# Hybrid decoder layer on one core: down groups added to x2 in DRAM by accumulating DMAs, and the gate of two up groups 15 products later

## The chip, the cores and the metric

The kernel runs on one core of a Trainium2 chip. The metric is the device time of one execution in microseconds (us). The engines are named as the profile names them: PE (TensorE, with PEld for its weight loads), DVE (VectorE), ACT (ScalarE), POOL (GpSimd) and SP (SyncE, which here only issues DMAs). Each engine runs its own instructions in the order of the program, and waits for others by semaphores.

## The reference

One layer of a decoder: sequence 512, width 2048, all float32. The first half (a combined projection, attention heads and SSD heads, an output projection) is not touched by the change. What matters here is the second half:

```
x = x + concat(attn, ssm) @ w_out                      # this sum is "x2" below
h = rms_norm(x, norm2_w)
u = causal_dwconv(h @ w_up, ffn_conv_w, ffn_conv_b)    # w_up: 2048 x (2 * 5632), conv of 3 taps
u_gate, u_val = split(u, 2)
return x + (silu(u_gate) * u_val) @ w_down             # w_down: 5632 x 2048
```

## The kernel before, in words

Everything is held transposed, with channels on the 128 partitions and the 512 positions along the free axis. x2 consists of 16 tiles of 128 x 512. Each is stored to DRAM when it is made (`x2d`, line 919), because it is needed again at the very end.

Each large product of the second half is computed twice over with a trick. First, every float32 operand is split into a rounded part `hi` (ACT copies and rounds, lines 1088 and 1145) and the rest `lo` (DVE subtracts, lines 1097 and 1146), and a product is hi*hi + hi*lo + lo*hi on PE (lines 1372, 1373, 1375). Second, blocks of 2 x 2 are multiplied by a Strassen-Winograd scheme: seven products, named P1 to P7, instead of eight. So a **group** is seven products of one 256-row block of output channels with both halves of the positions. It needs four weight tiles (DMAs by SP, line 1056), three sums of them on DVE (`s1`, `s2`, `s4`: lines 1067, 1070/1077, 1075) and one on POOL (`s3`, line 1063), and for each product one hi and one lo. A product is 24 matmuls of 128 x 256 where the contraction has 8 chunks, and 21 where it has 7.

The list `items` sets the order of the program by hand. For each group gi it runs P5(gi), P3(gi-1), P1(gi), P4(gi-1), P6(gi), P2(gi), P7(gi). The index of a product in this list is its **slot**. Work on the other engines is hung on slots by `at(slot, ...)`: `events` run before the lo of that slot, `after` behind it. In slot k the program issues the product, then what uses its result (`up_after` or `down_after`), the lo of product k+2, the work of `after`, and the hi of product k+3.

There are 44 **up groups** (0 to 43; each gives the gate channels and the value channels of one block of 128), and then 24 **down groups** in three passes of 8 (m = 0 to 7). Pass 0 contracts over the first 7 pairs of up blocks, pass 1 over the next 8, pass 2 over the last 7.

- `up_after` copies three of the products from PSUM with ACT (line 1227, tile `cP`) and adds the others with DVE. `up_side` then hangs the **gate** of the group on its slot t0 = slot of P4: two multiplies by the RMS factor (lines 1267, 1268), the convolutions (line 1246), the product (line 1257), and for each second group the Winograd sums of the pair (lines 890, 892, 893) and its store to DRAM (`gd`).
- At the start of a pass the right-hand operands of its products come back from `gd`: 14 loads into tiles `ld` (`b_load`, line 1134), each split into hi and lo (`b_split`, lines 1145 and 1146, tile `cmb`), 14 splits within 14 slots. Base is the slot of P5 of the group before the pass. In pass 0 there are three `ld` buffers, later five.
- `down_acc` allocates the accumulator of a down group (128 x 2 x 512) and loads into it x2 (pass 0, line 1284) or what the pass before left in DRAM (`pd`, line 1286). `down_after` adds each of the seven products into it with DVE straight from PSUM (line 1212). After P4 SP stores it to `pd`, or to the output in pass 2.
- Before the first up product, two right-hand operands (K22 and KT4) are still to be made from `xd` in DRAM: four loads (`x_load`, tile `ld`) and four splits (`x_split`, lines 1189 and 1190), at slots 2, 4, 5 and 6.

Of the kernel before, what the change touches and what calls it, by code (L numbers as in the profile page):

```python
# [187 lines left out]
def body(ctx, tc, xT, wi, wz, wo, wu, wd0, wd1, wd2, pp, pf, outT, dbg={}):  # L188
# [688 lines left out]

    x2d = [dram.tile([128, S], F32, name="x2d%d" % j) for j in range(NK)]
    xd = dram.tile([128, 8, 2, 256], F32, name="xd")
# [23 lines left out]
    def g_x2(acc, i):  # L903
# [14 lines left out]
        A_.activation(g[:, o:o + 2, :].rearrange("p a b -> p (a b)"), t, AF.Copy, scale=pc("nw2", j))  # L918
        nc.sync.dma_start(x2d[j], t)

# [10 lines left out]
        else:  # L931
# [10 lines left out]
            kind(KT3)  # L942
        yield
        square(t, i)
        if i + 4 < NK:
# [160 lines left out]
    for gi in range(len(groups)):  # L1106
# [6 lines left out]
        if gi:  # L1113
            at(p5 - 3 if gi > 1 else 1, add, gi, "s1", where=after)
            at(p5 - 3 if gi > 1 else 1, add, gi, "s3", where=after)
        else:
            at(0, add, gi, "s3", where=after)
# [37 lines left out]
    for p in range(len(PASSES)):  # L1155
# [10 lines left out]
        if p == 0:  # L1166
            at(base + 19, down_pool, where=after)

# [8 lines left out]
    def x_load(n):  # L1177
        if n < 4:
            x_ld.append(side_tile(box["pool"], [4, 256], "ld", 3))
            sy.dma_start(x_ld[n], xd[:, 4 * (n % 2):4 * (n % 2) + 4, n // 2, :])  # L1180
# [14 lines left out]

    for n, slot in enumerate((2, 4, 5, 6)):
        at(slot, x_split, n)


    box = {}  # L1200
    pds = [[dram.tile([128, 2, S], F32, name="pd%d_%d" % (p, m)) for m in range(8)] for p in range(2)]

    def down_after(g, x):
# [6 lines left out]
        if x == "P2":  # L1210
            src = src[:, lo]
        ve.tensor_tensor(a[:, row, half], src, a[:, row, half], op=op)  # L1212
        if g is groups[-1]:
            done = {"P7": (1, hi), "P3": (0, slice(0, S)), "P4": (1, lo)}.get(x)
            if done:
                sy.dma_start(outT[2 * g["m"] + done[0]][:, done[1]], a[:, done[0], done[1]])
        elif x == "P4":
            m, p = g["m"], g["p"]
            dst = pds[p][m] if p < 2 else outT[2 * m:2 * m + 2].rearrange("t p s -> p t s")
            at(pos[groups.index(g), "P4"] + 1, sy.dma_start, dst, a)  # L1220

# [16 lines left out]
    def up_side(i, ug, uv):  # L1238
# [20 lines left out]
        def t_sums(n):  # L1259
            sums(ve, box["gt"], n)  # L1260
            if n:
                pr = i // 2
                p = max(q for q in range(3) if PASSES[q][0] <= pr)
                at(t0 + (11 if i < NF - 1 else 9), sy.dma_start, gd[p][:, pr - PASSES[p][0]], box["gt"])

        t0 = pos[i, "P4"]
        for d, fn in ((0, lambda: ve.tensor_tensor(ug[:, 2:514], ug[:, 2:514], rbc, op=OP.mult)),
# [7 lines left out]
    def down_acc(gi):  # L1275
        g = groups[gi]
        m, p = g["m"], g["p"]
        if gi < NF + 2:
            a = g["acc"] = side_tile(lp, [2, S], "acc_s", 2)
        else:  # L1280
            a = g["acc"] = side_tile(box["pool"], [2, S], "acc", 4)
        if p == 0:
            for j in range(2):
                sy.dma_start(a[:, j, :], x2d[2 * m + j])
        else:
            sy.dma_start(a, pds[p - 1][m])

    for gi, g in enumerate(groups):
        if g["ph"] == "down":
            p5 = pos[gi, "P5"]  # L1290
            at(p5 - 2 if gi == NF else p5 - 5 if gi == NF + 1 else p5 - 2 if gi == NF + 2 else p5 - 6, down_acc, gi,
               where=after)

# [3 lines left out]
    def start_up():  # L1297
# [5 lines left out]
        for n in ("ug0", "uv0", "ug1", "uv1"):  # L1303
            box[n] = box["pool"].tile([128, 516], F32, name=n)
            ve.memset(box[n][:, 0:2], 0.0)
        x_load(0), x_load(1), x_load(2)

# [21 lines left out]
    p2["par"] = lp.tile([128, NPF], F32, name="par2")  # L1329
    sy.dma_start(p2["par"], pf)  # L1330
    last = g_x2(last_acc[0], NK - 1)
    split(1), split_lo(1)
# [13 lines left out]
    split_lo(3)  # L1346
    for _ in last:
        pass
    for k, (gi, x) in enumerate(items):
# [58 lines left out]
```

## Time and profile before

| | |
|---|---|
| median of the runs | 2079.29 us (3 runs, 2077.68 to 2079.3) |
| profiled execution, its own time | 2081.46 us |
| its span | 2079.7 us, granted clock 0.997 |
| busy: PE / DVE / ACT / POOL | 98% / 76% / 48% / 10% of the span |
| first half (span 0 to about 781 us) | not touched |
| up groups | about 781 to 1605 us |
| down passes 0, 1, 2 | from about 1622, 1775 and 1933 us |

How to read it: each engine's busy time is a share of the whole span. A wait is put down to the instruction that ended it. A stretch ("window") is given in us from the start of the span. In the rows of DVE one instruction begins a little before the end of the one before it is recorded, so the cost of one in a full queue is the distance from its start to the next start, which is about 0.08 us less than the duration shown.

### The profile page before, as it was taken

Reading aid. Unit: us, or ns where it says so; the run is one execution under the profiler, and the core shown is the slowest. Engines: PE = TensorE matmul, PEld = TensorE weight load, DVE = VectorE, ACT = ScalarE, POOL = GpSimd, SP = SyncE. Lnnn points to the kernel's source line nnn. Section 1 sums busy time; section 2 is a strip of 40 time slices with the busy share of each in tenths; the row PEclk is TensorE's granted clock in tenths of the full one; section 3 lists DMA queues with packets and bytes.
Section 4 is the critical chain, followed back from the end, with each engine's and each line's share of the span. In section 5 each row is a group of like instructions: output and inputs, shape, how many; then the busy total and the mean of one; then the engine's idle time right before and its main releaser. Section 6 shows DMA issues by size and latency. Waiting matters only on the chain.

```text
span 2079.7 us, 37702 instructions
## 1 busy us (share of the span) xinstructions
PE 2046.6 (98%) x15366; PEld 1932.4 (93%) x15366; DVE 1581.4 (76%) x2261; ACT 996.4 (48%) x1437; POOL 205.7 (10%) x108
## 2 busy tenths in 40 slices
PE   9999999999999999999999999999999899999999
PEld 7889888888888889999999999999999799999999
DVE  6545555345565558999999999999999977977976
ACT  6433435244444445555555555555555534634533
POOL 0020000000000001111111011101111111111110
PEclk9999999999999999999999999999999999999999
DMA  5233222332224556444444454454446667756763
GB/s 190 83 109 93 79 71 72 101 102 82 82 72 146 172 169 216 162 158 167 173 173 162 154 189 156 151 184 164 161 163 215 214 218 249 276 179 235 265 203 122
DMA packets 114684, 329.23 MB, mean 158 GB/s; under 512 B 10768, under 2 KB 35152, under 8 KB 111696
## 3 DMA queue, kind: packets, MB, share of 16 engines
q1 hardware_dynamic: 114512, 326.83, 46.9%
q8 instruction: 120, 1.97, 0.4%
q14 instruction: 52, 0.43, 0.1%
HBM read 284.81 MB, written 41.98 MB: 157 GB/s over the span
## 4 chain that ended last, share of the span: by engine, by line
PE 90%; DVE 5%; DMA 2%; issue 1%; ACT 1%; SPq 0%; POOL 0%; DVEq 0%; ACTq 0%; POOLq 0%
PE acc L183 30%; PE x L1373 16%; PE x L1372 16%; PE x L1375 16%; PE sm L183 4%; PE y L1373 3%; PE y L1375 3%; PE y L1372 3%; PE x L1364 2%; DVE lo L1097 1%; DVE cmb L1146 1%; DMA ld<-gd 1%; DMA t<-xT 1%; DVE lo L183 0%; DVE s L1067 0%
## 5 line engine op out<-in xcount | busy, mean ns | idle before, releaser
L1373 PE MATMUL x<-cmb,hi 128*128 128x256 f32 x3054 | 717.3, 278 | 9.9 <-DVE cmb L1146 9.9
L1372 PE MATMUL x<-cmb,hi 128*128 128x256 f32 x3054 | 717.4, 278 | 7.3 <-DVE acc L1212 2.7
L1373 PEld LDWEIGHTS x<-cmb,hi 128*128 128x128 f32 x3054 | 575.3, 188 | 12.1 <-DVE cmb L1146 12.0
L1372 PEld LDWEIGHTS x<-cmb,hi 128*128 128x128 f32 x3054 | 575.2, 188 | 8.9 <-issue 4.1
L1375 PE MATMUL x<-cmb,lo 128*128 128x256 f32 x3054 | 413.2, 277 | 1.9 <-DVE lo L1097 1.8
L1375 PEld LDWEIGHTS x<-cmb,lo 128*128 128x128 f32 x3054 | 377.6, 188 | 2.7 <-DVE lo L1097 2.7
L183 DVE TENSOR_TENSOR lo<-raw,hi 128x512 fp32r<-128x512 f32 (+1 forms) x240 | 164.4, 691 | 230.0 <-ACT hi L183 213.3
L1088 ACT ACTIVATE hi<-s 128x1024 fp32r<-128x1024 f32 (+1 forms) x201 | 201.0, 1000 | 285.2 <-DVE s L1067 192.3
L183 PE MATMUL acc<-A,hi 128*128 128x512 f32 x704 | 278.9, 396 | 1.8 <-ACT hi L183 1.8
L1063 POOL TENSOR_TENSOR rawb<-rawa,rawb 128x1024 f32<-128x1024 f32 (+1 forms) x67 | 167.3, 2497 | 1101.2 <-DVE s L1067 1066.7
L183 PE MATMUL acc<-A,lo 128*128 128x512 f32 x704 | 275.3, 391 | 0.1
L183 PE MATMUL acc<-B,hi 128*128 128x512 f32 x704 | 274.5, 390 | 0.0
L183 ACT ACTIVATE hi<-raw 128x512 fp32r<-128x512 f32 (+1 forms) x240 | 150.0, 629 | 239.1 <-PE acc L183 202.6
L1097 DVE TENSOR_TENSOR lo<-s,hi 128x1024 fp32r<-128x1024 f32 (+1 forms) x201 | 238.1, 1185 | 15.5 <-issue 14.0
L1097 DVE TENSOR_TENSOR lo<-rawa,hi 128x1024 fp32r<-128x1024 f32 (+1 forms) x203 | 240.1, 1183 | 0.0
L1088 ACT ACTIVATE hi<-rawa 128x1024 fp32r<-128x1024 f32 (+1 forms) x203 | 208.7, 1029 | 38.0 <-PE x L1373 37.9
L183 PEld LDWEIGHTS acc<-A,lo 128*128 128x128 f32 x704 | 132.2, 188 | 29.8 <-DVE lo L183 1.8
L183 PEld LDWEIGHTS acc<-A,hi 128*128 128x128 f32 x704 | 132.5, 188 | 28.1 <-ACT hi L183 2.7
L183 PEld LDWEIGHTS acc<-B,hi 128*128 128x128 f32 x704 | 132.4, 188 | 25.9 <-DVE B L183 0.3
L1227 ACT ACTIVATE cP<-x 128x256 f32<-128x256 f32 x132 | 50.6, 384 | 198.1 <-PE x L1375 198.1
L183 PE MATMUL acc<-hi,A 128*128 128x256 f32 (+2 forms) x448 | 135.5, 302 | 0.7 <-DVE u L183 0.7
L183 PE MATMUL acc<-lo,A 128*128 128x256 f32 (+2 forms) x448 | 133.5, 298 | 0.0
(224 smaller groups left out, 2884.0 us busy)
## 6 DMA issues: line engine op xcount, KB each, us to landing
rawa<-wu SPq DMA_DIRECT2D x175, 512.0 KB, 3.7
raw<-wi SPq DMA_DIRECT2D x79, 512.0 KB, 3.6
rawa<-wd SPq DMA_DIRECT2D x64, 448.0 KB, 4.2
rawb<-wu SPq DMA_DIRECT2D x44, 512.0 KB, 4.5
gd<-gt SPq DMA_DIRECT2D x22, 1024.0 KB, 4.6
raw<-wo SPq DMA_DIRECT2D x32, 512.0 KB, 3.5
rawa<-wd SPq DMA_DIRECT2D x32, 512.0 KB, 4.1
ld<-gd SPq DMA_DIRECT2D x27, 512.0 KB, 5.9
```

Source lines behind the costliest of these rows:

```text
L183: return fn(out, *args, **kw)
L1063: (po if gi else ve).tensor_tensor(r, raw[gi, "11"][:, :n], r, op=OP.subtract)
L1088: se.activation(h[:, :n], src[:, :n], AF.Copy)
L1097: ve.tensor_tensor(l[:, :n], src[:, :n], h[:, :n].bitcast(F32), op=OP.subtract)
L1146: ve.tensor_tensor(lo, ld[:, :m, :], hi.bitcast(F32), op=OP.subtract)
L1227: se.activation(g[x], X[:, 256:] if x == "P5" else X[:, :256], AF.Copy)
L1364: pe.matmul(out, a[:, q * 128:(q + 1) * 128], b[:, q, :], start=False, stop=last and q == n - 1, skip_group_check=True)
L1372: pe.matmul(out, w, bk[:, 0, q, :], start=fresh and q == 0, stop=False, skip_group_check=True)
L1373: pe.matmul(out, w, bk[:, 1, q, :], start=False, stop=False, skip_group_check=True)
L1375: pe.matmul(out, l[:, q * 128:(q + 1) * 128], bk[:, 0, q, :], start=False, stop=q == n - 1, skip_group_check=True)
```

## The change

- **Deposits.** `x2d` becomes 8 tiles of 128 x 2 x 512, one for each m. The `pd` tiles go. For the down groups of passes 0 and 1 and for m = 0, 1, 2 of pass 2 (19 groups, `DEPOSIT`), nothing is loaded into the accumulator. The products that come first into a quarter of it (P5, P1, P6, P4) are copied from PSUM by ACT, and P2, P7, P3 are added by DVE as before. After P4 a DMA issued from POOL with `accum_op=add` adds the accumulator to `x2d[m]` in DRAM. For the three groups of pass 2 SP then copies `x2d[m]` to the output, DRAM to DRAM, six slots after P4. The last five groups of pass 2 load `x2d[m]`, add all seven products with DVE, and store to the output.
- **Gate.** For up groups 42 and 43, t0 is 15 slots later. Pair 21, which they form, is read in pass 2 only.
- **Buffers.** Because the up pool now lives until base + 36 (before: base + 19), the accumulators of the first five down groups come from tiles of the long-lived pool (`acc_s`) and, for the third, from an `ld` tile of the up pool.
- **Start of the up groups.** The first `x_load` goes into an `acc_s` tile and is issued before the last x2 tile is finished; its split moves from slot 2 to slot 3. The last square for the RMS sum goes through PSUM, and its add on DVE moves behind slot 2. `s3` of group 1 on POOL moves from slot 1 to slot 7.

```diff
-    x2d = [dram.tile([128, S], F32, name="x2d%d" % j) for j in range(NK)]
+    x2d = [dram.tile([128, 2, S], F32, name="x2d%d" % j) for j in range(NK // 2)]
...
+        if i == NK - 1:
+            q = box["ps"].tile([128, 512], F32, name="y")
+            A_.activation(q, t, AF.Square)
+            yield
+            V.tensor_tensor(p2["ssq"], p2["ssq"], q, op=OP.add)
+            return
         square(t, i)
...
-            at(p5 - 3 if gi > 1 else 1, add, gi, "s3", where=after)
+            at(p5 - 3 if gi > 1 else 7, add, gi, "s3", where=after)
...
-            at(base + 19, down_pool, where=after)
+            at(base + 36, down_pool, where=after)
...
-            x_ld.append(side_tile(box["pool"], [4, 256], "ld", 3))
+            x_ld.append(side_tile(box["pool"], [4, 256], "ld", 3) if n else side_tile(lp, [4, 256], "acc_s", 2))
...
-    for n, slot in enumerate((2, 4, 5, 6)):
+    for n, slot in enumerate((3, 4, 5, 6)):
         at(slot, x_split, n)
...
-    pds = [[dram.tile([128, 2, S], F32, name="pd%d_%d" % (p, m)) for m in range(8)] for p in range(2)]
+    DEPOSIT = lambda g: g["p"] < 2 or g["m"] < 3
...
-        ve.tensor_tensor(a[:, row, half], src, a[:, row, half], op=op)
+        if DEPOSIT(g) and x in ("P5", "P1", "P6", "P4"):
+            se.activation(a[:, row, half], src, AF.Copy)
+        else:
+            ve.tensor_tensor(a[:, row, half], src, a[:, row, half], op=op)
...
-            m, p = g["m"], g["p"]
-            dst = pds[p][m] if p < 2 else outT[2 * m:2 * m + 2].rearrange("t p s -> p t s")
-            at(pos[groups.index(g), "P4"] + 1, sy.dma_start, dst, a)
+            m, end = g["m"], pos[groups.index(g), "P4"]
+            out = outT[2 * m:2 * m + 2].rearrange("t p s -> p t s")
+            if DEPOSIT(g):
+                po.dma_start(x2d[m], a, accum_op=OP.add)
+                if g["p"] == 2:
+                    at(end + 6, sy.dma_start, out, x2d[m])
+            else:
+                at(end + 1, sy.dma_start, out, a)
...
-                at(t0 + (11 if i < NF - 1 else 9), sy.dma_start, gd[p][:, pr - PASSES[p][0]], box["gt"])
+                at(t0 + (11 if i < NF - 1 else 10), sy.dma_start, gd[p][:, pr - PASSES[p][0]], box["gt"])
 
-        t0 = pos[i, "P4"]
+        t0 = pos[i, "P4"] + (15 if i >= NF - 2 else 0)
...
-        if gi < NF + 2:
+        if gi < NF + 5 and gi != NF + 2:
             a = g["acc"] = side_tile(lp, [2, S], "acc_s", 2)
+        elif gi == NF + 2:
+            a = g["acc"] = side_tile(box["pool"], [2, S], "ld", 3)
         else:
             a = g["acc"] = side_tile(box["pool"], [2, S], "acc", 4)
-        if p == 0:
-            for j in range(2):
-                sy.dma_start(a[:, j, :], x2d[2 * m + j])
-        else:
-            sy.dma_start(a, pds[p - 1][m])
+        if not DEPOSIT(g):
+            sy.dma_start(a, x2d[m])
...
-        x_load(0), x_load(1), x_load(2)
+        x_load(1), x_load(2)
...
     sy.dma_start(p2["par"], pf)
+    x_load(0)
```

Three places show how the order on the engines moves. The first is DVE at the start of pass 0, from the lo of a weight sum to the first split of the fourth operand (KT1 to KT4 and K11 to K22 are the tiles `cmb`; `tg`, `tv`, `gt`, `ug`, `uv` belong to the gate; `acc_s` is a down accumulator). Before:

```order
L1212 TENSOR_TENSOR acc_s<-x,acc_s 128x256
L1075 TENSOR_TENSOR s<-s,rawa 128x896
L1097 TENSOR_TENSOR lo_17607<-rawa,hi_17580 128x896
L1146 TENSOR_TENSOR cmb_17534<-ld,cmb_17534 128x768
L1246 SCALAR_TENSOR_TENSOR tg<-ug_7204,par_7109,tg 128x512
L1233 TENSOR_TENSOR ug_7208<-x,cP_17489 128x256
L1097 TENSOR_TENSOR lo_17641<-rawa,hi_17612 128x1024
L1146 TENSOR_TENSOR cmb_17643<-ld,cmb_17643 128x1024
L1246 SCALAR_TENSOR_TENSOR tv<-uv_7206,par_7109,tv 128x512
L1212 TENSOR_TENSOR acc_s<-x,acc_s 128x256
L1097 TENSOR_TENSOR lo_17678<-s,hi_17650 128x896
L1146 TENSOR_TENSOR cmb_17643<-ld,cmb_17643 128x768
```

Two gate rows and two accumulator rows stand among the weights' lo and the operand splits. The same stretch of DVE in the changed kernel (line numbers there are 6 to 14 higher):

```order
L1081 TENSOR_TENSOR s<-s,rawa 128x896
L1103 TENSOR_TENSOR lo_17576<-rawa,hi_17549 128x896
L1152 TENSOR_TENSOR cmb_17508<-ld,cmb_17508 128x768
L1247 TENSOR_TENSOR ug_7185<-x,cP_17464 128x256
L1103 TENSOR_TENSOR lo_17609<-rawa,hi_17580 128x1024
L1152 TENSOR_TENSOR cmb_17611<-ld,cmb_17611 128x1024
L1103 TENSOR_TENSOR lo_17642<-s,hi_17614 128x896
L1152 TENSOR_TENSOR cmb_17611<-ld,cmb_17611 128x768
```

The two rows of `tg` and `tv` and the two of `acc_s` are gone from here; the gate rows stand behind the last split of the pass, and the two accumulator rows are ACT copies.

The second place is POOL in pass 0 of the changed kernel, where before there are only the `s3` rows (rawb<-rawa,rawb):

```order
L1069 TENSOR_TENSOR rawb<-rawa,rawb 128x896 x2
L1230 DMA x2d_140<-acc_s 128x1024
L1069 TENSOR_TENSOR rawb<-rawa,rawb 128x896
L1230 DMA x2d_141<-acc_s 128x1024
L1069 TENSOR_TENSOR rawb<-rawa,rawb 128x896
L1230 DMA x2d_142<-ld 128x1024
```

Between each two `s3` there is now one accumulating DMA, and the `s3` that follows it belongs to the group that starts three slots later.

The third place is ACT at the start of the up groups (`cP` are copies of products, `cmb` is the first operand made by `x_split`). Before:

```order
L1088 ACTIVATE hi_7228<-rawb 128x1024
L1189 ACTIVATE cmb_7259<-ld 128x1024
L1088 ACTIVATE hi_7266<-s 128x1024
L1227 ACTIVATE cP_7292<-x 128x256
L1088 ACTIVATE hi_7299<-acc_s 128x1024
```

In the changed kernel:

```order
L1094 ACTIVATE hi_7202<-rawb 128x1024
L1094 ACTIVATE hi_7235<-s 128x1024
L1241 ACTIVATE cP_7261<-x 128x256
L1195 ACTIVATE cmb_7267<-acc_s 128x1024
L1094 ACTIVATE hi_7274<-acc_s 128x1024
```

The split of the first operand, which reads what a DMA brings, has gone from ahead of a hi and a copy to behind them.

More of the change, by code (lines that the diff above doesn't have):

```diff
@@ L918, in g_x2 @@
         A_.activation(g[:, o:o + 2, :].rearrange("p a b -> p (a b)"), t, AF.Copy, scale=pc("nw2", j))
-        nc.sync.dma_start(x2d[j], t)
+        nc.sync.dma_start(x2d[j // 2][:, j % 2], t)
         def kind(k):
@@ L1290, in body @@
             p5 = pos[gi, "P5"]
-            at(p5 - 2 if gi == NF else p5 - 5 if gi == NF + 1 else p5 - 2 if gi == NF + 2 else p5 - 6, down_acc, gi,
-               where=after)
+            at(p5 - (1 if DEPOSIT(g) else 6), down_acc, gi, where=after)
     up_stack = ExitStack()
@@ L1346, in body @@
     split_lo(3)
-    for _ in last:
-        pass
+    next(last)
+    at(2, lambda: list(last), where=after)
     for k, (gi, x) in enumerate(items):
```

## The prediction

> **What bounds the kernel now.** I read the page's busy times first, then the stretches, then what PE and DVE waited for, then DVE's groups in one stretch.
>
> ```profile
> PE 2046.6 (98%) x15366; PEld 1932.4 (93%) x15366; DVE 1581.4 (76%) x2261; ACT 996.4 (48%) x1437; POOL 205.7 (10%) x108
> ```
>
> PE is the bound, so only time in which PE starves can be won. The stretches show where that is (PE busy with its matmuls, PEld, DVE, ACT, POOL, granted clock, DMA share, GB/s):
>
> ```profile
> 1440.00:1520.00 80.00, 80.00 (x708) 80.00 (x707) 75.48 (x94) 40.68 (x53) 9.83 (x4) 1.00 0.46 158
> 780.00:820.00 40.00, 37.66 (x319) 37.22 (x319) 34.90 (x46) 23.23 (x31) 6.88 (x4) 1.00 0.68 237
> 1600.00:1680.00 80.00, 68.16 (x542) 65.38 (x542) 74.26 (x96) 43.77 (x52) 9.40 (x3) 0.96 0.62 212
> 1760.00:1820.00 60.00, 56.65 (x470) 55.74 (x469) 55.02 (x65) 35.27 (x36) 10.04 (x3) 0.97 0.75 260
> 1920.00:1980.00 60.00, 57.12 (x488) 56.09 (x487) 54.50 (x69) 33.05 (x37) 8.70 (x3) 1.00 0.74 245
> 1840.00:1920.00 80.00, 80.00 (x707) 80.00 (x706) 59.71 (x72) 31.83 (x31) 9.62 (x4) 1.00 0.64 219
> ```
>
> The first row is PE at its pace: 708 matmuls in 80 us, 0.113 us each. I count what is missing at that pace, which takes in the slower matmuls around a wait. Start of pass 0: 708 - 542 = 166, or **18.8 us**. Pass 1: 531 - 470 = 61, **6.9 us**. Pass 2: 531 - 488 = 43, **4.9 us**. Start of the up groups: 354 - 319 = 35, of which some five are the twice as long matmuls of the stage before, **3.4 us**. Together 34.0 us; elsewhere in these two stages PE runs at its pace, as the last row shows for pass 1. The kernel cannot come far below 2079 - 34 = 2045.
>
> ```profile
> PE x L1373 <- DVE cmb L1146: 9.9, 10, 2.0
> PE x L1372 <- DVE acc L1212: 2.7, 4, 1.2
> PE y L1373 <- DVE cmb L1146: 2.4, 2, 2.0
> PE x L1372 <- ACT cP L1227: 2.3, 1, 2.3
> PE x L1375 <- DVE lo L1097: 1.8, 1, 1.8
> PE x L1372 <- DVE acc_s L1212: 1.8, 2, 1.1
> ```
>
> At the passes PE waits for DVE: for the splits of the operands (L1146), the lo, and the accumulation that frees its PSUM tile (L1212). The one wait for ACT is that of the up start. So the question is how long DVE's queue is at each start of a pass.
>
> **Pass 0.** DVE's groups from 1611.9, when the last-but-one up group's P4 is out, to the last split at 1658.3 (busy us, mean ns; only those that move):
>
> ```profile
> L1246 DVE SCALAR_TENSOR_TENSOR tg<-ug,par,tg 128x512 f32<-128x512 f32 x4 | 3.0, 746 | 1.5 <-ACT tg L1245 1.5
> L1246 DVE SCALAR_TENSOR_TENSOR tv<-uv,par,tv 128x512 f32<-128x512 f32 x3 | 2.2, 743 | 0.0
> L1257 DVE TENSOR_TENSOR gt<-tg,tv 128x512 f32<-128x512 f32 x2 | 1.4, 692 | 0.1
> L1267 DVE TENSOR_TENSOR ug<-ug,rbc 128x512 f32<-128x512 f32 x2 | 1.4, 685 | 0.0
> L1268 DVE TENSOR_TENSOR uv<-uv,rbc 128x256 f32<-128x256 f32 x2 | 0.8, 418 | 0.0
> L1212 DVE TENSOR_TENSOR acc_s<-x,acc_s 128x256 f32<-128x256 f32 x6 | 2.5, 416 | 0.0
> ...
> L1146 DVE TENSOR_TENSOR cmb<-ld,cmb 128x768 fp32r<-128x768 f32 x6 | 5.7, 951 | 0.2 <-ACT cmb L1145 0.2
> ```
>
> The queue is 46.4 us long, with 1.7 us of gaps (1.5 and 0.2). Back to back an instruction costs about 0.08 less than its mean. The gate of groups 42 and 43 that lies in it goes: 6 of L1246 (4 tg and 2 tv; one tv only touches the end) x 0.66 = 4.0; one L1257 0.61 (the other is group 41's); two L1267 1.2; two L1268 0.68: 6.5 in all. Four of the six L1212 become ACT copies (P5, P1, P6, and P5 of the next group): 1.34. The wait of 1.49 for ACT's `tg` goes with the gate. 46.4 - 9.3 = **37.1 us** stay. PE, at its pace, wants the last split after five products of 24 matmuls, eight of 21, and eight matmuls of the ninth: 296 x 0.113 = **33.4 us**. So DVE is 13.0 us late there now, and will be 3.7.
>
> The remaining 18.8 - 13.0 = 5.8 us arise behind the last split:
>
> ```profile
> 1666.44 2.23 DVE L893 TENSOR_TENSOR gt<-gt 128x256 f32<-128x256 f32 x1
> 1666.21 2.17 POOL L1063 TENSOR_TENSOR rawb<-rawa,rawb 128x896 f32<-128x896 f32 x1 [20.34 <-DVE s L1067]
> 1675.28 0.42 DVE L1212 TENSOR_TENSOR acc<-x,acc 128x256 f32<-128x256 f32 x1 [2.95 <-DMA acc<-x2d]
> ```
>
> These are the end of the same gate, a DVE instruction stretched to 2.23 us beside one of POOL, and a wait for x2 that the deposit no longer has. All go. In their place the gate runs from 18 to 35 slots behind the base, about 4.3 us of DVE for a group and 1.4 for the pair's sums. A group of down products takes 7 x 21 x 0.113 = 16.6 us of PE and then needs 7 lo, 3 sums and 3 adds, 7.0 + 3.0 + 1.0 = 11.0 us of DVE, so 15.3 and 16.7 with the gate: full, but each lo has a slot and two thirds of slack. I allow 0.6. Pass 0 loses 3.7 + 0.6 = 4.3 after: **-14.5 us**. If the cover fails, the gate costs what overflows, 1 to 3 us.
>
> **Passes 1 and 2.** DVE's L1212 alone in the stretches in which it has no gap (busy, count, clock, DMA share, GB/s):
>
> ```profile
> 1767.40:1799.60 32.20, 3.81 (x10) 0.95 0.95 328
> 1925.00:1960.00 35.00, 4.95 (x12) 1.00 0.89 298
> ```
>
> About five of 10 and six of 12 become ACT copies, 1.7 and 2.0 us. But DMA is nearly full there too, and a split that comes sooner may only wait for its load. On the other side, the granted clock halves once behind the waits:
>
> ```profile
> 1640.00:1646.80 6.80, 4.76 (x23) 4.46 (x23) 6.80 (x9) 3.25 (x4) 4.16 (x1) 0.50 0.71 232
> 1793.60:1797.00 3.40, 3.40 (x18) 3.40 (x18) 3.40 (x4) 2.25 (x3) 1.78 (x1) 0.50 1.05 400
> ```
>
> The 3.4 us at half cost 1.7 in pass 1, and may go with a shorter wait. I take **-2.0** for pass 1 and **-1.7** for pass 2, with bounds 0 and -5.
>
> **Start of the up groups.** DVE, ACT and PE in order of time:
>
> ```profile
> 790.87 1.23 DVE L1067 TENSOR_TENSOR s<-rawb,rawa 128x1024 f32<-128x1024 f32 x1
> ...
> 792.71 1.06 ACT L1189 ACTIVATE cmb<-ld 128x1024 fp32r<-128x1024 f32 x1 [0.67 <-DMA ld<-xd]
> 793.67 1.00 ACT L1088 ACTIVATE hi<-s 128x1024 fp32r<-128x1024 f32 x1
> 794.58 0.38 ACT L1227 ACTIVATE cP<-x 128x256 f32<-128x256 f32 x1
> 795.00 0.39 PE L1372 MATMUL x<-cmb,hi 128*128 128x256 f32 x1 [2.34 <-ACT cP L1227]
> ```
>
> The copy that PE waits for stood behind a hi and a split that waited for its load. The split now stands behind the copy. The weight sum that the hi reads ends at 792.1, 0.6 sooner without the square's add that DVE did ahead of it; a hi later, at 792.4 to 793.0 instead of 794.58, comes the copy: 1.6 to 2.2 us, **-1.8 us** of the 2.34. `s3` of group 1, six slots later, still has a slot until its hi; 2.4 us of POOL hide it.
>
> **What is added.** 76 ACT copies at the price of L1227:
>
> ```profile
> L1227 ACT ACTIVATE cP<-x 128x256 f32<-128x256 f32 x132 | 50.6, 384 | 198.1 <-PE x L1375 198.1
> pd<-acc SPq DMA_DIRECT2D x14, 512.0 KB, 3.6
> acc<-pd SPq DMA_DIRECT2D x16, 512.0 KB, 6.4
> q1 hardware_dynamic: 114512, 326.83, 46.9%
> 1702.94 2.13 POOL L1063 TENSOR_TENSOR rawb<-rawa,rawb 128x896 f32<-128x896 f32 x1 [14.62 <-DVE s L1067]
> ```
>
> 76 x 0.384 = 29 us of ACT, over passes in which it is busy about half the time: hidden, and the price is a PE wait where a copy queues behind a split that waits for its load, as at 794.58; up to 2.3 each.
>
> No accumulating DMA, and none issued by POOL, stands in this trace. Its **landing** lies between a store (3.6) and a load and a store in a row (6.4 + 3.6 = 10.0). The first reuse of an accumulator is 11 slots, 26 us, behind its deposit: hidden at both ends. Its **engine time**: 0.469 x 2079.7 us moved 326.83 MB, so 512 KB is 1.56 us of all 16 engines; a deposit is between one such piece and two. The load and the store it replaces are two, so the traffic is even or falls by 1.56 a group. I take two, the nearest to reading twice and writing once. Its **hold on POOL** lies between the 0.3 us of an issue on SP and the landing, 10.0. The `s3` behind it is wanted seven slots, 16.6 us, later; less its own 2.13 and the copy's wait, 13 us are free, and the row shows POOL idle for 14.62. Nothing at either end.
>
> A POOL instruction beside DVE did stretch one of DVE (the row of 1666.44). The Trainium skill ("SBUF — State Buffer", "Who interferes with whom") says that a DVE instruction with two SBUF inputs contends with a GpSimd one that reads SBUF, not with one that only writes, as a writer of descriptors does; by that the deposits stretch nothing. Were each to cost DVE such a 1.8 us, it would eat the 1.34 that the copies give a group.
>
> **Sum.** 14.5 + 2.0 + 1.7 + 1.8 = 20.0. The profiled execution took 2081.5 us (span 2079.7), so 2061.5; the median of the runs lies 2.2 lower: **2059**.
>
> **Rivals.**
> *Less gain.* The loads become the limit once DVE is faster.
>
> ```profile
> ld<-gd SPq DMA_DIRECT2D x27, 512.0 KB, 5.9
> ACT cmb L1145 <- DMA ld<-gd: 6.4, 6, 1.7
> ```
>
> Pass 0 has three `ld` buffers, so each split waits for the load that the third split before it set free: 5.9, then ACT and DVE 2.1 (an ACT split of this shape is the row of 792.71). Three such rounds, 24 us, from the fifth split, which by the sum above ends near 1629, reach 1653 where PE wants the last at 1611.9 + 33.4 = 1645.3: pass 0 keeps 8, and passes 1 and 2 gain nothing, DMA being at 0.95 and 0.89. For it: ACT waited for `ld` six times around pass 0. Against: DVE hardly did (0.2), and loads there can land sooner than the median of all passes. 18.8 - 8 + 1.8 = 12.6 gained: 2067.
>
> *All starvation gone.* PE's waits get so short that neither the half clock (3.4 + 1.7 us lost by the rows above) nor the slow matmuls come back; pass 0 keeps 2, pass 1 1.5, pass 2 1, the start 0.5: 29 gained, 2050. The Trainium skill ("TensorE: Matmul & The Clock Gate", "What's actually happening") has the clock halve after an idle window of about 3.4 us; by that it would not halve any more, where here it did after gaps of about 2.
>
> *No change.* The copies on ACT come as late as DVE's adds, so the PSUM waits (2.7 + 1.8) grow while the split waits shrink: within 4 us of before.
>
> *Slower.* A deposit takes more of the DMA engines than load and store together. In pass 1 away from its start they are idle 36% of 80 us, 6.9 us a group; with the 3.1 set free, 10 us of engine time a deposit are the point from which each further us costs one in each of 19 groups. At 12: 38 - 20, so 2097. Speaking for it: the kind is unknown here. Against: it needs over six times a plain transfer.
>
> **How the numbers follow.** Forecast 0.50, less gain 0.22, all gone 0.14, no change 0.06, slower 0.08. A measurement of this kernel can tell about 0.2% (4.2 us) from no change. Faster is the first three, 0.86; same 0.06; slower 0.08. The likeliest's own range is 2054 to 2065. The range for 8 in 10 reaches beyond its two neighbours: 2048 to 2074.
>
> **What would show it.** Right: in 1600 to 1680 over 660 matmuls (that is 5 us missing); no gate row on DVE between the splits of pass 0; waits for `cmb` down from 12 us to under 6; the copy of the up start before its split, and PE's wait there under 1 us; POOL idle for several us between deposit and next `s3`; no half clock near 1640. Wrong: PE waiting for ACT copies of accumulators, for `rawb` by way of POOL, or DMA near 1.0 through pass 1; any of these would put the time above 2065.

## The result, and the profile after

The changed kernel takes **2064.31 us** (median of 6 runs, 2063.12 to 2066.1) where the kernel before takes 2079.3 (2077.68 to 2082.71): **0.9928 of before, 95% interval 0.9916 to 0.9941**, faster by 15.0 us. The forecast was 2059, with a range of 2048 to 2074. The sign and most of the steps came as predicted; 5 us of the 20 did not come.

The profiled execution has a span of 2064.1 us. Its page gives the busy times:

```profile
PE 2041.0 (99%) x15366; PEld 1929.7 (93%) x15366; DVE 1556.5 (75%) x2185; ACT 1018.4 (49%) x1513; POOL 221.9 (11%) x127
```

76 instructions went from DVE to ACT (2261 to 2185, 1437 to 1513), and 19 deposits came to POOL (108 to 127). The stretches that the prediction counted, in the changed kernel (columns as there; the last one 10 us earlier, since the stage comes earlier):

```profile
780.00:820.00 40.00, 38.15 (x323) 37.74 (x323) 35.83 (x47) 23.34 (x31) 6.75 (x3) 1.00 0.68 241
1600.00:1680.00 80.00, 75.46 (x635) 74.60 (x635) 73.47 (x87) 48.44 (x66) 12.52 (x6) 0.98 0.64 199
1760.00:1820.00 60.00, 57.09 (x484) 55.81 (x483) 50.51 (x51) 36.73 (x45) 11.31 (x7) 1.00 0.75 231
1910.00:1970.00 60.00, 57.96 (x504) 57.37 (x504) 51.07 (x58) 36.91 (x50) 13.57 (x8) 1.00 0.85 246
```

At 0.113 us a matmul, pass 0 now misses 708 - 635 = 73 matmuls, 8.2 us (18.8 before); pass 1 misses 47, 5.3 us (6.9); pass 2 misses 27, 3.1 us (4.9). What PE waited for in the whole span, by engine and line, as total us, count and longest:

```profile
PE x L1386 <- DVE cmb L1152: 8.6, 10, 1.6
PE x L1385 <- ACT cP L1241: 1.5, 1, 1.5
PE y L1386 <- DVE cmb L1152: 0.8, 1, 0.8
```

The waits for accumulators (4.5 us before) are gone up to the last five groups, which still add with DVE and keep their 1.2 us; there is none for an ACT copy of one. The waits for the operands' splits have only gone from 12.3 to 9.4 us.

All kernels here run the same 15366 matmuls in the same order, so a second count needs no windows: the time between the starts of the same two matmuls in two traces. The table gives it for the 4270th to the 4700th (start of the up groups), the 11190th to the 12300th (pass 0), the 12300th to the 13300th (pass 1) and the 13900th to the 15000th (pass 2), less the same time in the kernel before. "First half" is all ahead of the 4270th; there the kernels differ in little more than where the x2 stores go, and in two stores more with the deposits twice. Negative is faster, in us:

```
                             first half  up start  pass 0  pass 1  pass 2   median us  ratio (95% interval)
changed kernel                  -1.8       +0.4    -10.6    -1.6    -1.9     2064.31   0.9928 (0.9916-0.9941)
gate only (old start)           -2.1       -0.3     -9.4    -0.1     0.0     2070.43   0.9955 (0.9942-0.9967)
deposits only (old start)       -2.8       +1.1     -5.0    -2.2    -1.9     2071.05   0.9961 (0.9948-0.9975)
old start of the up groups      -2.6       +1.0    -10.8    -2.2    -1.5     2065.76   0.9933 (0.9920-0.9945)
copies on DVE                   -1.5       +0.3     -8.6    +0.2     0.0     2070.04   0.9954 (0.9942-0.9967)
s3 later on POOL                -1.1       +0.6     -9.9    -2.2    -1.9     2066.09   0.9933 (0.9921-0.9946)
s1 behind the splits            -2.0        0.0     -9.3    -2.2    -1.9     2066.49   0.9930 (0.9917-0.9942)
four ld buffers                 -1.9       +0.3    -14.1    -1.6    -1.5     2062.00   0.9910 (0.9896-0.9924)
x load behind weight loads      -2.3       -0.9    -11.4    -2.2    -1.9     2064.15   0.9924 (0.9910-0.9937)
deposits twice                  -0.2       -0.3    -12.6    -0.8    -0.4     2067.62   0.9938 (0.9926-0.9951)
plain stores                    -1.3       +0.4    -11.4    -1.7    -1.9     2065.85   0.9932 (0.9920-0.9945)
four ld buffers + x load        -1.9       -1.5    -14.1    -2.2    -1.5     2060.08   0.9905 (0.9892-0.9919)
the same + sums later           -1.4       -0.8    -14.9    -2.2    -1.9     2060.59   0.9906 (0.9891-0.9921)
```

The changed kernel's span is 15.6 us shorter, of which 13.8 lie in these stages: the profiled execution of the kernel before took 1.8 us longer in the first half, and up to 2.8 longer than the others. The medians, from other executions, give 15.0. Where several rows have the same order of work in a stage (pass 0 of the changed kernel, of the old start, of `s3` later, of the x load and of the plain stores: 10.6, 10.8, 9.9, 11.4, 11.4), their spread shows what one execution can tell: 1 to 1.5 us.

### The profile page after: what moved, and what is told of

It is laid out like the page before. It is cut to its first block, busy times and chain, and to the rows that moved or that the text cites. A ratio compares the mean times of both kernels' runs of the same rounds, so it can differ in the third digit from the quotient of the medians.

```text
span 2064.1 us, 37659 instructions
## 1 busy us (share of the span) xinstructions
PE 2041.0 (99%) x15366; PEld 1929.7 (93%) x15366; DVE 1556.5 (75%) x2185; ACT 1018.4 (49%) x1513; POOL 221.9 (11%) x127
## 4 chain that ended last, share of the span: by engine, by line
PE 94%; DVE 3%; DMA 1%; issue 1%; ACT 1%; SPq 0%; POOL 0%; DVEq 0%; ACTq 0%; POOLq 0%
PE acc L183 31%; PE x L1386 16%; PE x L1388 16%; PE x L1385 16%; PE sm L183 4%; PE y L1386 3%; PE y L1388 3%; PE y L1385 3%; PE x L1377 2%; DVE cmb L1152 1%; DVE lo L1103 1%; DMA ld<-gd 0%; DMA rawa<-wu 0%; DVE lo L183 0%; DMA raw<-wi 0%
## 5 line engine op out<-in xcount | busy, mean ns | idle before, releaser
L183 PE MATMUL acc<-hi,B 128*128 128x256 f32 (+2 forms) x448 | 132.7, 296 | 0.0
```

Source lines behind the costliest of these rows:

```text
L183: return fn(out, *args, **kw)
```

## The experiments

**Gate or deposits.** Each of the two main edits alone, both with the start of the up groups as before. The first:

```diff
-        t0 = pos[i, "P4"]
+        t0 = pos[i, "P4"] + (15 if i >= NF - 2 else 0)
```

> The kernel before with one of the three edits: only the gate of the two last up groups 15 slots later (with the accumulators of the first five down groups in the buffers that this needs). No deposit, no edit at the start of the up groups. Theory (the gain is DVE's queue at the start of pass 0, of which the gate is the larger part): pass 0 regains the gate's 6.5 to 8 us and perhaps the half clock of 3.4 us there, nothing changes in passes 1 and 2; 2069 to 2073 us, 0.995 to 0.997 of before. Rival (the copies and deposits do it, since the gate is only moved to another full place): within 2 us of before, 1.000. Second rival (the gate alone carries the whole gain of pass 0): 2068 or less.

With it go the buffers that it needs, and the two loads of x2 for an accumulator become one. The second is the changed kernel with this line taken back, and with it the same buffers and the edit of the start:

```diff
-        t0 = pos[i, "P4"] + (15 if i >= NF - 2 else 0)
+        t0 = pos[i, "P4"]
```

> The changed kernel with the gate back at its old slots and the start of the up groups as before: only deposits and ACT copies. Theory: passes 1 and 2 gain the 1.6 and 1.8 us that the changed kernel's trace shows there, pass 0 gains the adds of its queue (1.3) and the 2 to 3 us of the wait for x2; 2073 to 2075 us, 0.997 to 0.998. Rival (the lighter DMA traffic, 308 for 327 MB, speeds up the whole stage, and the gate little): 2066 to 2069, 0.994. If the parts only work together, the sum of the gains of this run and of the gate alone falls short of 15 us.

2070.43, as the theory had it, and 2071.05, less than either reading of the second run had (2073 to 2075, or 2066 to 2069): its pass 0 gains 5.0 where 3.3 to 4.3 were expected. Pass 0 and pass 1, first with the gate alone, then with the deposits alone:

```profile
1600.00:1680.00 80.00, 75.11 (x627) 73.52 (x627) 75.85 (x97) 45.35 (x53) 10.56 (x4) 0.98 0.64 219
1760.00:1820.00 60.00, 56.36 (x470) 55.27 (x469) 53.31 (x62) 32.52 (x32) 8.07 (x3) 0.97 0.72 252
```

```profile
1600.00:1680.00 80.00, 71.61 (x587) 69.20 (x586) 73.82 (x90) 47.27 (x63) 12.07 (x6) 0.98 0.63 196
1760.00:1820.00 60.00, 57.03 (x488) 55.75 (x488) 52.05 (x52) 38.70 (x47) 12.56 (x6) 1.00 0.79 243
```

The gate alone takes pass 0 from 542 to 627 matmuls and leaves pass 1 at its 470. The deposits alone take pass 0 to 587 and pass 1 to 488. So passes 1 and 2 belong to the deposits, and pass 0 mostly to the gate. There the parts do not add up: 9.4 and 5.0 alone, 10.6 together. Something else holds pass 0 at about 8 us of loss once the queue is shorter.

**Copies or traffic.** What in the deposits helps, DVE's shorter queue or the lighter DMA traffic?

```diff
-            se.activation(a[:, row, half], src, AF.Copy)
+            ve.tensor_copy(a[:, row, half], src)
```

> The changed kernel with the 76 first contributions copied by DVE, not by ScalarE: deposits without relief of DVE's queue but for the x2 waits. Theory (the gains of passes 1 and 2, 1.6 and 1.8 us, and over 1 us of pass 0 are DVE's shorter queue): 4 to 5 us more than the changed kernel, 2068 to 2070. Rival (these gains come from the loads of accumulators that are gone, i.e. the DMAs, and DVE's adds lay in its idle time): within 1 us of the changed kernel, 2063.5 to 2066.

2070.04, 5.7 us more than the changed kernel, where the theory had 4 to 5. Passes 1 and 2 lose their whole gain (+0.2 and 0.0 in the table), with the deposits and their lighter traffic still there; the stretches have 471 matmuls in pass 1, where the kernel before has 470:

```profile
1600.00:1680.00 80.00, 74.72 (x622) 73.65 (x621) 75.17 (x97) 44.10 (x53) 12.52 (x6) 0.96 0.61 192
1760.00:1820.00 60.00, 55.14 (x471) 53.86 (x470) 53.73 (x62) 34.48 (x34) 12.70 (x6) 1.00 0.75 231
```

The half clock of pass 1 (1793.6 before) is gone here too, so that is not where the gain lies. What helps is that the copies are not on DVE. The deposit earns its keep because it turns an add into a copy, which ACT can do.

**What a deposit costs.** Once twice as many, the second into a scratch tile; once a plain store in its place, from the same queue.

```diff
                 po.dma_start(x2d[m], a, accum_op=OP.add)
+                po.dma_start(x2e, a, accum_op=OP.add)
```

> The changed kernel with every deposit issued twice, the second into a scratch tile in DRAM that two more stores of 256 KB fill ahead of the up groups. Prices one deposit more per group: 3.3 us of DMA engine time and 0.9 us of POOL each, 19 times. Theory (deposits lie beside other work): within 2 us of the changed kernel, 2064 to 2067, POOL still idle ahead of each s3, DMA share in the passes up by 0.1 to 0.14. Rival (deposits delay the loads of the splits at the starts of passes 1 and 2, where the share is already 0.75 to 0.85): 1 to 3 us more in each of these passes, 2067 to 2071. Rival (each is a direct price): 19 x 3.3 = 62 us more.

```diff
-                po.dma_start(x2d[m], a, accum_op=OP.add)
+                po.dma_start(x2d[m], a)
```

> The changed kernel with every deposit a plain store from the same queue, without accumulation: x2 and the sums of the earlier passes are lost from the result, the work of all engines but the DMAs stays. Price of accumulating: by the changed kernel's trace a deposit takes 3.3 us of DMA engine time, a plain piece 1.6. Theory (deposits are nearly hidden, and doubling them cost about 3 us through the split loads of passes 1 and 2): 0 to 2 us less than the changed kernel, 2062.5 to 2064.5, pass 1 and 2 losing 0 to 1 us less each. Rival (accumulation holds POOL or the accumulators and so costs several us): 2060 or less.

2067.62, just above the theory's range and in that of the delayed loads, and 2065.85, above the range expected. Accumulating costs this kernel nothing that these runs can tell: with the plain store no stage differs by more than 0.8 us, within the spread. In the changed kernel (the page's queue with packets, MB and share of the engines, and its transfer with the median landing; then POOL in order of time):

```profile
q0 software_dynamic: 2736, 9.96, 3.0%
x2d<-acc POOLq DMA_DIRECT2D x14, 512.0 KB, 5.4
```

```profile
1772.79 0.89 POOL L1230 DMA_DIRECT2D x2d<-acc  x1 [12.05 <-DMA rawa<-wd]
1777.37 4.38 POOL L1069 TENSOR_TENSOR rawb<-rawa,rawb 128x1024 f32<-128x1024 f32 x1 [3.68 <-DVE s L1073]
```

And with plain stores:

```profile
q0 software_dynamic: 2736, 9.96, 1.2%
x2d<-acc POOLq DMA_DIRECT2D x14, 512.0 KB, 3.1
```

```profile
1772.56 0.59 POOL L1230 DMA_DIRECT2D x2d<-acc  x1 [12.03 <-ACT acc L1219]
```

A deposit takes 0.030 x 2064.1 / 19 = 3.3 us of engine time where the plain store takes 0.012 x 2063.8 / 19 = 1.3; it lands in 5.4 us for 3.1, and holds POOL for 0.89 for 0.59. All of that is covered: POOL has 3.7 us to spare behind it. The cover has an end, though. With two deposits a group the starts of passes 1 and 2 give back 0.8 to 1.4 and 1.0 to 1.5 us, where the DMA share rises from 0.75 to 0.87 and from 0.84 to 0.95:

```profile
1760.00:1820.00 60.00, 56.47 (x476) 54.95 (x476) 49.95 (x50) 35.80 (x44) 13.49 (x9) 1.00 0.87 256
1910.00:1980.00 70.00, 67.41 (x579) 66.48 (x578) 57.91 (x67) 41.44 (x55) 17.60 (x12) 1.00 0.95 275
```

In pass 1 ACT's splits now wait for their loads, which they do not in the changed kernel (the waits of that stretch):

```profile
ACT cmb L1154 <- DMA ld<-gd: 2.4, 2, 2.1
```

So 19 more deposits cost 3.3 us by the medians, 2.4 when each median is set against the kernel before that ran beside it (the intervals overlap), and not 62.

**What holds pass 0.** In the changed kernel DVE's queue there has two holes and one stretched split. The waits of 1600 to 1680, then DVE, POOL and PE in order of time:

```profile
ACT cmb L1151 <- DMA ld<-gd: 4.7, 4, 2.1
DVE cmb L1152 <- ACT cmb L1151: 1.4, 2, 0.7
```

```profile
1629.56 1.22 DVE L1152 TENSOR_TENSOR cmb<-ld,cmb 128x1024 fp32r<-128x1024 f32 x1 [0.72 <-ACT cmb L1151]
...
1635.13 2.95 POOL L1069 TENSOR_TENSOR rawb<-rawa,rawb 128x896 f32<-128x896 f32 x1 [17.48 <-DMA ld<-gd]
1636.18 0.38 PE L1386 MATMUL x<-cmb,hi 128*128 128x256 f32 x1 [1.40 <-DVE cmb L1152]
1636.81 2.08 DVE L1152 TENSOR_TENSOR cmb<-ld,cmb 128x768 fp32r<-128x768 f32 x1 [0.69 <-ACT cmb L1151]
1638.95 0.58 PE L1386 MATMUL x<-cmb,hi 128*128 128x256 f32 x1 [1.60 <-DVE cmb L1152]
```

Twice DVE waits for ACT, which waits for a load. The split at 1636.81 takes 2.08 us for its 0.95: until 1638.1 POOL is at the difference `s3`. PE waits for just this split, the tenth of 14, and for the ninth (before that 0.69 us for the fourth and 0.85 for the eighth); the last four come in time. Three suspects: the loads, POOL, and the place of the weight sum in the middle of the queue.

The loads, by a fourth buffer (in the tiles named `ld` of pool `up` too), so that each load goes out one split earlier:

```diff
-        box["depth"] = 3
+        box["depth"] = 4
...
-        early = 5
+        early = 6 if p == 0 else 5
...
-            at(... base + slots[q - (5 if p else 3)] + 1, b_load, k0 + q)
+            at(... base + slots[q - (5 if p else 4)] + 1, b_load, k0 + q)
```

> The changed kernel with four ld buffers in pool up for three: each load of pass 0 is issued one split earlier. Theory of the loads (the 'less gain' rival: the split loads are the limit of pass 0): DVE's two waits behind ACT's splits (0.72 and 0.69) go, pass 0 loses 6 to 7 us for 8.2; 2062 to 2063 us. Theory of the queue's middle (PE wants the splits of P2 and P7 of the first down group 24 us into the queue and DVE needs 28 to bring them; load waits are 1.4 of the 4.4): the same direction, at most 1.4 us, and the three PE waits of 0.85, 1.40 and 1.60 shrink by that sum. If nothing is gained, the waits for loads only took the place of others.

2062.00. Pass 0 gains 14.1 us, and it loses 708 - 666 = 42 matmuls, 4.7 us:

```profile
1600.00:1680.00 80.00, 77.27 (x666) 76.39 (x665) 75.20 (x92) 49.59 (x67) 13.44 (x6) 1.00 0.63 200
```

Its waits in that stretch, and DVE and POOL in order of time:

```profile
PE x L1386 <- DVE cmb L1152: 2.7, 4, 1.4
ACT cmb L1151 <- DMA ld<-gd: 0.4, 1, 0.4
```

```profile
1633.97 2.09 DVE L1152 TENSOR_TENSOR cmb<-ld,cmb 128x1024 fp32r<-128x1024 f32 x2
1634.20 3.85 POOL L1069 TENSOR_TENSOR rawb<-rawa,rawb 128x896 f32<-128x896 f32 x1 [16.67 <-DVE s L1073]
```

DVE does not wait for ACT any more. But the pair of splits beside `s3` is not stretched either (2.09 for two), and now POOL takes 3.85 where it took 2.95 (2.13 in the row of 1702.94). So the fourth buffer took away two things, and the expected "at most 1.4 us" was too small.

POOL, by the same `s3` five slots later:

```diff
-            at(p5 - 3 if gi > 1 else 7, add, gi, "s3", where=after)
+            at(p5 + 2 if gi == NF + 1 else p5 - 3 if gi > 1 else 7, add, gi, "s3", where=after)
```

> The changed kernel with one weight difference on POOL (s3 of the second down group) five slots later, behind the last splits of pass 0, so that no POOL instruction runs beside them. Theory (one split stretched from 0.95 to 2.08 us beside POOL holds PE up in a row of waits and brings the half clock): 1.1 us of DVE and up to 1.7 us of half clock less, 2061.5 to 2063.5 us. Rival (the waits there are set by the loads of ld, so the split only waits elsewhere): 2064, within 0.5 us of the changed kernel; the stretch goes, the waits for ld grow.

2066.09, and the edit did not do what it was made for:

```profile
1636.26 2.95 POOL L1069 TENSOR_TENSOR rawb<-rawa,rawb 128x896 f32<-128x896 f32 x1 [17.64 <-DVE s L1073]
1638.31 1.71 DVE L1152 TENSOR_TENSOR cmb<-ld,cmb 128x768 fp32r<-128x768 f32 x1 [1.06 <-ACT cmb L1151]
```

Nothing else stands in POOL's own order between the two places, so `s3` began as soon as its sum on DVE was done, as before. The run is a repeat of the changed kernel and by itself decides nothing on POOL.

The weight sum, with `s1` and `s3` behind the two splits of their slot in all three passes:

```diff
+            if q == 9:
+                at(base + 11, add, g0 + 1, "s1", where=after)
+                at(base + 11, add, g0 + 1, "s3", where=after)
```

> The changed kernel with the weight sum s1 (1.09 us of DVE) and difference s3 of the second down group of each pass issued behind the two splits of their slot, not ahead of them. Theory of the queue's middle: PE's waits for the ninth and tenth split shrink by up to 1.1 us in each pass (3 passes), 2061 to 2062.5 us. Theory of the last split (as the prediction had it: the length of the whole queue decides): nothing changes, 2064 to 2066. Theory of the loads: in pass 0 the splits would wait for their loads instead, passes 1 and 2 might gain 1 each.

2066.49: no gain. In pass 0 the splits, now wanted sooner, wait for their loads instead:

```profile
ACT cmb L1152 <- DMA ld<-gd: 6.9, 5, 2.0
DVE cmb L1153 <- ACT cmb L1152: 3.5, 4, 1.2
```

ACT's wait goes from 4.7 to 6.9 and DVE's from 1.4 to 3.5. Passes 1 and 2 gain nothing that the spread of the table can tell. That is the outcome of the loads: with three buffers the middle of the queue is not what holds pass 0. With four it was not tried. The run also does what the one before was made for: `s3` runs from 1638.18 to 1640.30 beside no split, no split is stretched, and yet pass 0 gains only 9.3. POOL alone is not what holds it either.

How much of the fourth buffer's gain is loads and how much POOL? Two other traces help, with pass 0 as in the changed kernel. With the x load moved, the second split of the pair lost to POOL:

```profile
1633.23 3.99 DVE L1152 TENSOR_TENSOR cmb<-ld,cmb 128x1024 fp32r<-128x1024 f32 x2
1633.46 2.95 POOL L1069 TENSOR_TENSOR rawb<-rawa,rawb 128x896 f32<-128x896 f32 x1 [17.49 <-DVE s L1073]
```

The plain stores show the same pair, 3.99 beside 2.95; both gain 11.4 in pass 0. With two deposits a group it went as with four buffers, and pass 0 gained 12.6:

```profile
1636.01 2.09 DVE L1155 TENSOR_TENSOR cmb<-ld,cmb 128x1024 fp32r<-128x1024 f32 x2
1636.24 3.85 POOL L1072 TENSOR_TENSOR rawb<-rawa,rawb 128x896 f32<-128x896 f32 x1 [17.58 <-DVE s L1076]
```

What separates that trace's pass 0 from 14.1 is in part the wait for loads that it still has (0.8 us on DVE). DVE's queue, measured as the prediction did it, is 39.3 us long in the changed kernel, 38.1 here and 36.6 with four buffers. In the changed kernel too, 3.99 us pass from the start of the pair's first split to the end of the second (1634.90 to 1638.89), so the second wait for a load is hidden behind POOL there. Of the 2.7 us some 1.9 hang on who goes first at that place, DVE or POOL, and some 0.7 on the first wait for a load.

Who goes first follows the loads in the traces at hand. In the seven in which POOL goes first, the kernel with the gate alone among them, ACT's part of the second split, which waits for the load, ends between 1.0 us behind and 0.3 us ahead of the end of the first split on DVE. In the six in which DVE does, among them the kernel before and all three with four buffers, it ends 0.4 to 2.2 us ahead. So a split that is not ready in time lets POOL in, and the fourth buffer brings it in time. That is an order found in thirteen traces; POOL and the loads were not changed apart.

**The start of the up groups.** The changed kernel with the old start, and the changed kernel with its one load in another place:

> The changed kernel with the start of the up groups as it was (square, x load, its split and s3 of the first groups at their old places). Theory (in the changed kernel the copy comes before its split, but the weight load now comes later, so the edit of the start is worth 0.5 us at most): 2064 to 2065 us, the same as the changed kernel within 0.7 us. Prediction's step (1.8 us): 2066. Rival (the edit of the start costs, by the later weight load): 2063.

```diff
-    x_load(0)
     last = g_x2(last_acc[0], NK - 1)
...
     for slot in range(min(events), 0):
         run(slot)
+    x_load(0)
     split(3)
```

> The changed kernel with the first x load issued behind the weight loads of the second up group, not ahead of them. Theory (the prediction's 1.8 us at the start of the up groups is lost since the weight sum now waits 1.17 us for its load): that wait goes, the copy that PE waits for comes up to 1.2 us sooner, PE's wait of 1.53 falls under 0.6; 2063 us. Rival (the load is late for another reason, or the split of x is then late): nothing gained, PE's wait stays or moves to the split; 2064 to 2066.

2065.76 and 2064.15: the first lies nearer the prediction's step than the theory, the second in the range of its rival, but such times cannot tell one us. In the changed kernel, DVE, ACT and PE:

```profile
789.68 1.23 DVE L1073 TENSOR_TENSOR s<-rawb,rawa 128x1024 f32<-128x1024 f32 x1 [1.17 <-DMA rawa<-wu]
791.93 0.38 ACT L1241 ACTIVATE cP<-x 128x256 f32<-128x256 f32 x1
792.36 0.38 PE L1385 MATMUL x<-cmb,hi 128*128 128x256 f32 x1 [1.53 <-ACT cP L1241]
```

The copy does stand ahead of the x split now, but the sum that its queue hangs on waits 1.17 us for a weight load, which went out on SP behind the moved x load. With that load behind the weight loads:

```profile
788.22 1.23 DVE L1073 TENSOR_TENSOR s<-rawb,rawa 128x1024 f32<-128x1024 f32 x1
790.90 0.39 PE L1385 MATMUL x<-cmb,hi 128*128 128x256 f32 x1 [0.49 <-ACT cP L1241]
```

The wait for the load is gone and PE's wait is 0.49 for 1.53. The stage can be told by the traces: with the old start 0.0 (the kernel before), -0.3, +1.0 and +1.1; with the changed start between -0.3 and +0.6 in seven traces; with the load behind -0.9, -1.5 and -0.8 in three. In the two old starts at +1.0 and +1.1 the granted clock was 0.5 for 3.4 us from 793.3 and 793.5, behind the wait; in no other trace was it so.

A second loss lies behind that wait. In the changed kernel, DVE, POOL and PE:

```profile
800.47 2.88 DVE L1196 TENSOR_TENSOR cmb<-ld,cmb 128x1024 fp32r<-128x1024 f32 x1 [0.29 <-ACT cmb L1195]
799.88 2.39 POOL L1069 TENSOR_TENSOR rawb<-rawa,rawb 128x1024 f32<-128x1024 f32 x1
804.54 1.22 PE L1388 MATMUL x<-cmb,lo 128*128 128x256 f32 x8 [0.33 <-DVE lo L1103]
```

Beside `s3` of group 1 at its new place the third split of x takes 2.88 us for its 1.21, the lo behind it comes late, and PE waits for it. From the 4270th to the 4450th matmul the changed kernel is 0.9 us ahead of the kernel before, and the three with the x load behind are 1.9 ahead. From there to the 4690th all ten traces with the changed start lose 0.5 to 1.3, the other three with the old start at most 0.1. With the old start `s3` stretches a split too (2.31 us in the kernel before), but PE does not wait. That the new slot of `s3` alone does it was not tried.

**Both repairs**, and then the sums of the last pair but one 14 slots later as well, 1.5 us of DVE out of pass 0's queue:

```diff
+        late = 14 if i == NF - 3 else 0
...
-            at(t0 + 7, t_sums, 0, where=after), at(t0 + (10 if i < NF - 1 else 8), t_sums, 1, where=after)
+            at(t0 + 7 + late, t_sums, 0, where=after), at(t0 + late + (10 if i < NF - 1 else 8), t_sums, 1, where=after)
```

> The changed kernel with both repairs: four ld buffers in pass 0, and the first x load behind the weight loads. Theory: the gains of the two (2.3 to 3.5 us in pass 0, 1 us at the start of the up groups) add up: 2060 to 2061.5 us. Rival (one of them was noise of single executions): 2062 or more.

> Both repairs, and the sums and store of the last pair but one 14 slots later, 1.5 us of DVE (0.68, 0.41 and 0.42) that stand in the first 11 us of pass 0's queue. Theory (with the loads in time, DVE's queue is what PE waits for in pass 0): 1 to 1.5 us less than with both repairs alone, 2059 to 2060.5 us. Rival (with four buffers the loads are still the limit, or pass 0's loss is now in the slow matmuls behind any wait): the same as with both repairs.

**2060.08** and 2060.59: 0.9905 (0.9892 to 0.9919) and 0.9906, the first as expected, the second as its rival had it. Both repairs add up, and the runs (2059.45 to 2060.83) lie below all of the changed kernel's. With the sums later, pass 0 gains another 0.8 us in the trace (673 matmuls for 666), which the medians do not show.

## Why the prediction was right, and where it was not

- **PE is the bound and only starvation can be won: right.** The gain lies in the counted places; from the 4700th to the 11190th matmul the traces agree.
- **Pass 0, -14.5: mis-sized, it gave 9.9 to 11.4.** The step that failed is "37.1 us stay". What goes from the queue was counted rightly: with the loads in time and POOL giving way, 36.6 us stay, and pass 0 gains 14.1 and loses 4.7, where the sum had 14.5 and 4.3. But the sum took the rest of the queue as back to back. It had 0.7 + 0.7 us of waits for loads and 1.1 of a split held by POOL. From the P4 row at 1610.5 to its last split at 1649.8 it is 39.3 us long. That makes DVE 5.9 us late at the last split, by the sum's own rule, of the 8.2 that pass 0 loses; the sum had 0.6 for the rest, and where its 2.3 lie was not followed. The rule also asked when PE wants the *last* split; PE waited longest for the ninth and tenth.
- **Rival *less gain*: its mechanism came true in part, in pass 0 only.** It had three buffers as the limit and 8 us of loss there; 8.2 were measured, and a fourth buffer took 3.5 of them. That the two figures agree is luck: its three rounds of 8 us put the last split at 1653, 41.1 us behind the P4 row, where 39.3 were measured, DVE waited 1.4 us in all, and it had no POOL in it. That passes 1 and 2 would gain nothing was wrong, and so the time came between it (2067) and the forecast.
- **Passes 1 and 2, -2.0 and -1.7: right** (-1.6 and -1.9), and for the reason given, the adds that leave DVE: with the copies on DVE both are 0.
- **Start of the up groups, -1.8: wrong.** It gave nothing that the traces can tell, by two steps that failed. The first took the weight sum to end 0.6 us *sooner*; it waited 1.17 us for its load, since the x load had been moved past that load on SP. Every queue that a moved step passes has to be followed. With that order mended PE is 1.9 us ahead behind the copy, what the sum had wanted. The second is "2.4 us of POOL hide it": `s3` at its new place holds a split on DVE for 1.7 us, and 0.5 to 1.3 are lost again. With the load behind, the edit is worth about 1.
- **What is added, nothing: right.** No wait for an accumulator copy on ACT; deposits of two pieces' engine time (3.3 us, estimated 3.1), landing between the bounds, hidden. The *slower* rival wanted 10 us of engine time for each.
- **Signs named beforehand.** No gate row among the splits, the copy of the up start ahead of its split, POOL idle for several us behind a deposit: seen. Over 660 matmuls in 1600 to 1680, split waits under 6 us, PE's wait at the start under 1 us: not in the changed kernel; the first in the versions with four buffers, the third in those with the x load moved, the second in none (6.9 to 7.4 us with four buffers). *All starvation gone* did not come.

The half clock near 1640 stayed, half as long as before:

```profile
1638.80:1642.20 3.40, 3.25 (x15) 3.25 (x16) 3.40 (x5) 2.62 (x4) 0.00 (x0) 0.50 0.79 251
```

It did not decide the loss: the kernel with the old start has no such stretch in pass 0 and gains the same (10.8). The Trainium skill ("TensorE: Matmul & The Clock Gate", "What's actually happening") has the clock halve after an idle window of about 3.4 us. Here it halved right behind waits of 1.40 and 1.60 with matmuls between them, so one idle stretch of that length is not needed.

On the deposits' rule the traces agree, but they test it little. No DVE instruction of the changed kernel's passes is stretched beside a deposit, but what stands beside each of the 19 is a lo, with a gate row at two of them and the end of a split at one. The split at 1636.81 stands beside POOL's subtraction, and that is the case which the Trainium skill ("SBUF — State Buffer", "Who interferes with whom") names: a DVE instruction with two SBUF inputs against a GpSimd one that reads SBUF. The measured rows are narrower than that rule. In the changed kernel a weight sum (L1083, from 1707.71) and a lo, which read two SBUF tiles each, run beside an `s3` (from 1707.29) in 1.09 and 1.08 us, no longer than elsewhere, and that `s3` takes 2.12. What sets the splits apart is not shown.

## What to carry to other kernels

When work is taken out of a full queue, do not price the rest as back to back: ask for each instruction that moves up whether its load and its buffer move up too, and which POOL instruction it will then stand beside. Two relieved parts that gain less together than alone (9.4 and 5.0 gave 10.6) say that a third limit stands behind, here three load buffers, and a POOL instruction that gets in where a split comes late. A first contribution that is copied and deposited by an accumulating DMA frees the add's engine, as long as the DMAs have room; what gained was the copy on the idle engine, not the traffic saved.

## What the runs showed of the hardware that was not expected

- An accumulating DMA of 512 KB took 3.3 us of engine time and landed in 5.4 us, against 1.3 and 3.1 for a plain store of the same tile from the same queue.
- A split on DVE and a subtraction on POOL hold each other up whole instructions long, and either can win: beside the same `s3` the pair of splits took 3.99 us and POOL 2.95, or the splits 2.09 and POOL 3.85. In thirteen traces DVE won where the second split was ready at least 0.4 us before the first ended, and POOL where it was not. Weight sums and lo rows beside an `s3` were not held up at all (1.09 and 1.08 us).
- An instruction moved later in POOL's own order, with nothing between the two places, started when its input was ready, as before: the place in a program sets the order on an engine, not the time.
